# An opening of a trunk layer in written order: modulation weights first, latent blocks of two value heads ahead of the context's, spectra spread anew

## The chip, the core and the metric

The kernel runs on one core of one Trainium2 chip. The core has five engines with instruction streams of their own: TensorE (PE, matmuls), VectorE (DVE), ScalarE (ACT), GpSimd (POOL) and SyncE (SP, which here issues the loads). The metric is the device time of one execution in microseconds (us). A matmul in this kernel multiplies a stationary 128x128 tile with up to 512 moving columns and adds into a bank of PSUM.

## The reference, cut to what matters

One layer of a hybrid block over 512 latent tokens and 256 context tokens of width 1024. What the change touches is the front of it:

```python
mod  = silu(c)     @ w_ada + b_ada          # shift, scale, ... of the latent
modc = silu(c_ctx) @ w_ada + b_ada          # the same of the context
hc = rmsnorm(ctx, norm1_g) * (1 + csc1) + csh1
h  = rmsnorm(x,   norm1_g) * (1 + sc1)  + sh1
khc, vhc, lgc = project_kvg(hc, ...)        # keys, values, gates of the context
kh,  vh,  lg  = project_kvg(h,  ...)        # and of the latent
q = silu(conv(h @ w_in[q] + b_in[q]))       # queries: latent only
# filters of the long convolution, from a small network of sines:
a = sin(fr * (z @ w1 + b1)); a = sin(fr * (a @ w2 + b2)); a = sin(fr * (a @ w3 + b3))
k = (a @ w4) * exp(-t * |decay|);  spec = rfft(k)      # 8 spectra: 2 orders x 4 column groups
```

Behind it follow a chunkwise linear attention (4 heads, both directions), the long convolutions by spectra, gated merge, output projection, SwiGLU and a last norm.

## The kernel before

All large products run in three matmuls: each fp32 operand is split into a high part (ScalarE copy, `hi`) and a low part (VectorE subtraction, `lo`), and hi x hi, lo x hi and hi x lo go to one PSUM bank. In the trace `wr` is a raw weight, `wh` and `wl` its parts, `hTh` and `hTl` the parts of one of the eight modulated latent tiles (128 of 1024 channels x 512 tokens), `hb` among others those of the context.

The opening does this. SyncE loads the vectors (`vecs`), small constants, x in four pieces (`uh`, `ul`), constant matrices (`mats`), the first half of the modulation weights in 16 pieces (`hTh`, `hTl` and `K` lend them their space), later the second half. `ada_first` multiplies a half by silu(c) (L337), copies the sums (L343), transposes them (L346) and adds bias and gain (`modT` L353, `amod` L354). `sq_sums` and `rms_bcast` make the norm: squares on ScalarE, adds on VectorE (L403), column sums (L406), a power on GpSimd (L391), a broadcast product (L393). `modulated` (L1094 to L1100) makes hTh and hTl of four tiles at a time, and `part` the projections of four query tiles, `qps`, with the 24 matmuls of a tile in triples k by k (`gemm`, L233 to L235). `filter_network` (L419 to L438) makes the filters' input, `filter_spectrum` (L453 to L507) one spectrum in three steps: products with w4, window and split; 36 matmuls with a DFT table; combination. `v_head` makes values (and for head 0 the gates, 272 columns) in six blocks of 128 tokens, four latent and two of the context; 24 matmuls each. Then come eight key tiles `k_tile` with the gate arithmetic `gate_math` behind the first.

The order on an engine is set by a scheduler: instructions are taken by priority and by hints (`tc.issue_after`, `tc.high_priority`), each engine runs its own list in that order, and a DMA waits in SyncE's list too. At most eight of SyncE's transfers are in flight; the ninth's issue waits until the first of them has landed.

Of the kernel before, what the change touches and what calls it, by code (L numbers as in the profile page):

```python
# [1 line left out]

# [157 lines left out]
def build(nc, tc, I, out, dbg=None):  # L160
# [33 lines left out]
    NQ, XA, AH, AQ, W0 = 4, (False, False), (2, 2), 2, (3, 0)  # L194
# [6 lines left out]
    def bank(p=None):  # L201
        return T(p or psH, [128, 512], F32, "bank")

# [57 lines left out]
    dma(vecs[:], I["vecs"])  # L261
# [13 lines left out]
    dve.tensor_scalar_mul(mngh[:], mng, 0.5)  # L275
    bhalf = T(P0, [128, 64], F32, "bhalf")
    dve.tensor_scalar_mul(bhalf[:], bin_, 0.5)
# [6 lines left out]
    def ada_prepare(p):  # L284
        nonlocal silc
        silc = T(p, [128, KT, 32], F32, "silc")
# [5 lines left out]
        dve.memset(silc[:], 0.0)  # L292
        dve.scalar_tensor_tensor(silc[:, :, 0:2], th[:], 1.0, cch[:], op0=ALU.add, op1=ALU.mult)
        cb2 = T(p, [128, 40], F32, "cb2")
# [38 lines left out]
    def ada_first(p, half, units, tag):  # L333
        ps = bank()
        for k in range(KT):
# [4 lines left out]
            if k < KT - 1:  # L340
                yield m.ins
        rows = T(p, [128, 512], F32, tag)
        copy = act.activation(rows[:, :256], ps[:, :256], AF.Copy)  # L343
        pt = bank()
        for j in range(2):
            mark = pe.transpose(pt[:, 128 * j : 128 * j + 128], rows[:, 128 * j : 128 * j + 128], ident)  # L346
# [7 lines left out]
        m = dve.scalar_tensor_tensor(amod[:, fs], modT[:, 1, fs], 1.0, n1g[:, fs], op0=ALU.add, op1=ALU.mult)  # L354
        yield mark.ins, m.ins, copy.ins
# [39 lines left out]
    def sq_sums(acc, x, k, nblk, p, tag, ps=None):  # L395
# [8 lines left out]
        if k == KT - 1:  # L404
            for b in range(nblk):
                pe.matmul(ps[:, b : b + 1], acc[:, 128 * b : 128 * b + 128], ones[:, 0:1], start=True, stop=True)  # L406
# [223 lines left out]
    dma(bgb[:], I["bg"].broadcast_to([128, 16]))  # L630

    NV = 258

    def v_weights(h):
        w = 272 if h == 0 else 256
        parts = []
        for kh in range(2):
            src = [(I["wv"][h, kh], slice(0, 256))]
            if h == 0:
                src.append((I["wg"][kh], slice(256, 272)))  # L640
            parts.append(wsplit(src, [128, 4, w]))
        return parts

    def v_head(p, h, parts):
        w = 272 if h == 0 else 256
# [3 lines left out]
        for b0 in range(0, 6, per):  # L649
# [20 lines left out]
            if h == 0:  # L670
                dve.tensor_add(gates[:, b0], ps[:, 256:272], bgb[:])
# [406 lines left out]
    with tc.issue_after(am):  # L1078
        list(e0)
# [530 lines left out]
```

## Time and profile before

| | |
|---|---|
| time, median of 3 runs | 1218.94 us (1218.71 to 1219.33) |
| profiled execution | 1219.83 us |
| its span, first to last instruction | 1218.0 us |
| mean granted TensorE clock | 0.992 |
| TensorE busy | 1180.8 us (97%) |
| VectorE busy | 833.2 us (68%) |
| ScalarE busy | 528.9 us (43%) |

The share of TensorE is an average: it is near 100% over most of the span and far lower in the first 36 us, where data arrive and small chains of steps on several engines precede the first projection. The other engines matter where TensorE waits for them.

### The profile page before, as it was taken

How to read it: one execution, taken by the hardware profiler on the slowest of the kernel's cores; microseconds unless marked ns; L12 is line 12 of the kernel's file. 1: busy time of each engine (PE TensorE's matmuls, PEld its weight loads, DVE VectorE, ACT ScalarE, POOL GpSimd, SP SyncE). 2: the span in 40 equal slices, each digit the busy share in tenths (PEclk: the TensorE clock that was granted, in tenths of full speed). 3: DMA queues.
4: the chain of work that ended last, by engine and by line, in shares of the span. 5: the costliest groups of instructions: out<-in, count | busy, mean ns of one | idle time of the engine just before them, and what ended most of it. 6: DMA issues, size and time to landing. Idle time of an engine off the chain costs nothing.

```text
span 1218.0 us, 16831 instructions
## 1 busy us (share of the span) xinstructions
PE 1180.8 (97%) x6440; PEld 1012.9 (83%) x6440; DVE 833.2 (68%) x1336; ACT 528.9 (43%) x824; POOL 87.7 (7%) x168
## 2 busy tenths in 40 slices
PE   4999999999999999999989999999999999999997
PEld 2799988888888888888778988889888888888886
DVE  5967797978989999897758896767753434432332
ACT  3754465753545444453655642333432232322221
POOL 0011110100010010101032031000000000000000
PEclk9999999999999999999989999999999999999998
DMA  9744453364244353434695686773443333233312
GB/s 346 248 159 163 136 185 106 133 237 143 75 162 137 130 174 102 147 106 155 211 319 180 196 265 218 260 234 121 140 138 104 90 100 101 85 95 96 96 48 70
DMA packets 63377, 189.04 MB, mean 155 GB/s; under 512 B 8760, under 2 KB 12608, under 8 KB 61120
## 3 DMA queue, kind: packets, MB, share of 16 engines
q1 hardware_dynamic: 51536, 150.20, 38.6%
q0 software_dynamic: 11760, 37.76, 8.7%
q8 instruction: 51, 0.84, 0.3%
q14 instruction: 30, 0.25, 0.1%
HBM read 154.37 MB, written 33.55 MB: 154 GB/s over the span
## 4 chain that ended last, share of the span: by engine, by line
PE 89%; DVE 4%; DMA 3%; ACT 2%; issue 1%; POOL 0%; SPq 0%; DVEq 0%; POOLq 0%; ACTq 0%
PE bank L233 26%; PE bank L234 26%; PE bank L235 26%; PE bank L659 2%; PE bank L660 2%; PE bank L661 2%; DMA wr<-qd 1%; DMA wr<-in_wph 1%; PE bank L616 1%; PE bank L463 1%; DVE wl L215 1%; PE bank L464 1%; ACT wh L214 1%; DMA ul<-in_xT 1%; PE bank L337 0%
## 5 line engine op out<-in xcount | busy, mean ns | idle before, releaser
L233 PE MATMUL bank<-hTh,wh 128*128 128x512 f32 (+1 forms) x952 | 366.6, 387 | 2.9 <-ACT hTh L1094 2.0
L234 PE MATMUL bank<-hTl,wh 128*128 128x512 f32 (+1 forms) x952 | 366.1, 386 | 2.9 <-DVE hTl L1100 2.2
L235 PE MATMUL bank<-hTh,wl 128*128 128x512 f32 (+1 forms) x952 | 365.6, 385 | 0.0
L214 ACT ACTIVATE wh<-wr 128x1024 fp32r<-128x1024 f32 (+1 forms) x167 | 172.2, 1033 | 400.8 <-PE bank L234 205.1
L215 DVE TENSOR_TENSOR wl<-wr,wh 128x1024 fp32r<-128x1024 f32 (+1 forms) x167 | 197.8, 1187 | 170.9 <-ACT wh L214 169.6
L233 PEld LDWEIGHTS bank<-hTh,wh 128*128 128x128 f32 x952 | 178.9, 188 | 37.5 <-ACT hTh L1094 2.2
L234 PEld LDWEIGHTS bank<-hTl,wh 128*128 128x128 f32 x952 | 179.0, 188 | 36.8 <-DVE hTl L1100 2.5
L235 PEld LDWEIGHTS bank<-hTh,wl 128*128 128x128 f32 x952 | 179.0, 188 | 34.6
L233 PE MATMUL bank<-big,wh 128*128 128x512 f32 (+1 forms) x266 | 94.7, 356 | 0.0
L234 PE MATMUL bank<-big,wh 128*128 128x512 f32 (+1 forms) x266 | 94.6, 356 | 0.0
L235 PE MATMUL bank<-big,wl 128*128 128x512 f32 (+1 forms) x266 | 94.6, 355 | 0.0
L372 DVE SCALAR_TENSOR_TENSOR wr<-wr,crow 128x1024 f32<-128x1024 f32 x32 | 38.9, 1218 | 28.3 <-DMA wr<-in_wada 28.2
L233 PEld LDWEIGHTS bank<-big,wh 128*128 128x128 f32 x266 | 50.3, 189 | 7.2
L235 PEld LDWEIGHTS bank<-big,wl 128*128 128x128 f32 x266 | 50.3, 189 | 7.1
L234 PEld LDWEIGHTS bank<-big,wh 128*128 128x128 f32 x266 | 50.3, 189 | 7.1
L214 ACT ACTIVATE hb<-hb 128x512 fp32r<-128x512 f32 (+1 forms) x49 | 36.5, 767 | 33.3 <-DVE hb L468 18.5
L1554 DVE TENSOR_TENSOR s<-s,bank 128x512 f32<-128x512 f32 x22 | 15.1, 686 | 46.4 <-PE bank L235 46.4
L391 POOL TENSOR_TENSOR rr<-rv,negh 128x2 f32<-128x2 f32 (+1 forms) x6 | 5.5, 924 | 510.7 <-DVE rv L389 510.7
L215 DVE TENSOR_TENSOR hb<-hb,hb 128x512 fp32r<-128x512 f32 (+1 forms) x49 | 40.4, 858 | 2.0 <-ACT hb L214 1.8
L659 PE MATMUL bank<-wh,hTh 128*128 128x256 f32 (+1 forms) x128 | 36.4, 285 | 0.0
L661 PE MATMUL bank<-wh,hTl 128*128 128x256 f32 (+1 forms) x128 | 36.4, 285 | 0.0
L660 PE MATMUL bank<-wl,hTh 128*128 128x256 f32 (+1 forms) x128 | 36.4, 284 | 0.0
(383 smaller groups left out, 2208.2 us busy)
## 6 DMA issues: line engine op xcount, KB each, us to landing
wr<-in_win SPq DMA_DIRECT2D x64, 512.0 KB, 3.8
wr<-in_w SPq DMA_DIRECT2D x60, 512.0 KB, 3.5
wr<-in_wada SPq DMA_DIRECT2D x32, 512.0 KB, 4.1
Kd<-K POOLq DMA_DIRECT2D x8, 1024.0 KB, 4.7
K<-Kd SPq DMA_DIRECT2D x8, 1024.0 KB, 6.4
wr<-in_wv SPq DMA_DIRECT2D x8, 512.0 KB
gmd<-s POOLq DMA_DIRECT2D x16, 256.0 KB, 2.5
wr<-in_wph SPq DMA_DIRECT2D x8, 512.0 KB, 4.2
```

What stands on the lines that cost most here:

```text
L214: act.activation(hi, x, AF.Copy)
L215: dve.tensor_sub(lo, x, hi.bitcast(F32))
L233: pe.matmul(o, wh, xh, start=first, stop=False)
L234: pe.matmul(o, wh, xl, start=False, stop=False)
L235: return pe.matmul(o, wl, xh, start=False, stop=last)
L372: dve.scalar_tensor_tensor(w, w, 1.0, crow[:], op0=ALU.mult, op1=ALU.mult, accum_out=s)
L463: pe.matmul(ps[:], lhs, w4h, start=True, stop=False)
L464: pe.matmul(ps[:], lhs, w4l, start=False, stop=True)
L659: pe.matmul(o, xh, wh, start=bool(k == 0), stop=False)
L660: pe.matmul(o, xh, wl, start=False, stop=False)
L661: m = pe.matmul(o, xl, wh, start=False, stop=bool(k == KT - 1))
L1554: dve.tensor_tensor(t[:], t[:], pb[:], op=ALU.mult)
```

## The change

Only the opening and the order of value heads and spectra are written anew; the arithmetic is the same, and the number of instructions of each engine too.

- A context manager `in_order` ties the instructions that are traced inside it, engine by engine, into the written order.
- SyncE's list: x and the vectors, constants, the first modulation half, four query weights, the network's weights, the second half, the context, then decay, w4 and DFT table of spectrum 0, then gate bias (`bgb`), value bias and value weights.
- Query projections: in `early_q` a matmul group takes one part of weights and one of hT, for half of the eight tiles; the groups with hTh come first. Weights are split in halves A and B. VectorE makes hTh of tiles 2 and 3. The network's first two layers and the second modulation half stand between these groups.
- The context's squares, norm and modulation are steps (`context`) between the blocks of the value heads. `v_head` is a generator: four latent blocks of head 0, two of head 1, then the context's two blocks of head 0 and one of head 1.
- Spectrum 0 opens behind head 0's last block; spectrum 1 follows at once, 2 in the middle of head 2, 3 and 4 behind heads 2 and 3; query tiles 0 and 1 are finished behind head 2.

```diff
+    @contextmanager
+    def in_order():
+        traced = nc.cur_bb.bb.instructions
+        n, last, ends = len(traced), {}, []
+        yield ends
+        for i in traced[n:]:
+            if i.engine in last:
+                tc.add_manual_dep(
+                    i, last[i.engine], mybir.DependencyInfo(mybir.DependencyClass.NoSync, mybir.DependencyReason.DATA), reason="in_order"
+                )
+            last[i.engine] = i.name
...
-                if half == 0 and (kp, a) == W0:
-                    dma(raws[0][:, :1024].rearrange("p (a b) -> p a b", a=KT), I["win"][FT_Q])
...
-    ada = ada_first(PH, 0, units[0], "s2")
-    for k in range(KT):
-        sq_sums(ax_, xt[k], k, 4, PH, "s2", sums)
-    next(network)
-    ahead(AH[0])
...
-    for i in range(AQ):
-        part(i, 0)
-    next(sp0)
-    ada = ada_first(PH, 1, units[1], "s2")
-    tr, am, copy = ahead(8)
...
+    def early_q(i, ks, w, x):
+        for k in ks:
+            count[i] += 1
+            m = pe.matmul(qps[i][:], early[i][w][:, k], hT[x][k][:], start=count[i] == 1, stop=count[i] == 3 * KT)
...
+    with in_order() as ends:
...
+        units = [ada_load(PH, 0, slots[0])]
+        for i in range(NQ):
+            dma(raws[i], I["win"][FT_Q + i])
+        dma(net[:, :772], I["net"])
+        units.append(ada_load(PH, 1, slots[1]))
...
+        early_q(0, (2, 0, 3, 1), 0, 0)
+        early_q(0, KA, 1, 0)
+        early_q(1, KA, 0, 0)
+        early_q(1, KA, 1, 0)
...
+        network = filter_network(PH, net)
+        next(network)
+        early_q(2, KA, 0, 0)
+        early_q(2, KA, 1, 0)
+        ada = ada_first(PH, 1, units[1], "s2")
...
+        early_q(1, KA, 0, 1)
+        ahead(4)
+        early_q(2, KA, 0, 1)
...
+                dma(bgb[:], I["bg"].broadcast_to([128, 16]))
+                v0 = v_head(PH, 0, v_bias(PH, 0), v_weights(0))
+                raws1, bias1 = v_load(1), v_bias(PH, 1)
...
+        rms_bcast(csums[:, :2], 2, cb_, PH, "s2")
+        next(v0)
+        raws2 = v_load(2)
+        bias2 = v_bias(PH, 2)
+        context(3)
+        next(v0)
+        context(1)
+        next(v0)
+        v1 = v_head(PH, 1, bias1, parts1)
+        context(4)
+        next(v1)
...
-    for h in range(NH):
-        v_head(PH, h, v_weights(h))
-        PR[0] = 600
-        if h:
-            q_late(PH, h - 1)
-        next_spectrum()
+    next_spectrum()
+    for h in range(2, NH):
+        v = v_head(PH, h, bias2, parts2) if h == 2 else v_head(PH, h, v_bias(PH, h), v_weights(h))
+        for i in range(6):
+            next(v)
+            if i == 3:
+                next_spectrum() if h == 2 else None
+        for i in range(2) if h == 2 else (h - 1,):
+            q_late(PH, i)
+        next_spectrum() if h == 2 else next_spectrum()
```

Three places show how the order moves. The first is SyncE's list at its start, before (`in_wada` are the modulation weights, `in_win` query weights, `in_hdec` a spectrum's decay):

```order
1 L261 DMA vecs_69<-in_vecs 128x380
2 L630 DMA bgb_89<-in_bg 128x16
3 L1013 DMA hb_118<-in_net 128x772
4 L1037 DMA uh_134<-in_xT 128x1024
5 L1037 DMA ul_136<-in_xT 128x1024
8 L1040 DMA mats_71<-in_mats 128x640
9 L328 DMA hTh_148<-in_wada 128x512
...
17 L328 DMA K_156<-in_wada 128x512 x4
18 L325 DMA wr_144<-in_win 128x1024
19 L328 DMA K_157<-in_wada 128x512 x4
```

And after:

```order
1 L1111 DMA uh_107<-in_xT 128x1024
2 L1111 DMA ul_109<-in_xT 128x1024
3 L1111 DMA uh_111<-in_xT 128x1024
4 L1115 DMA vecs_69<-in_vecs 128x380
5 L1111 DMA ul_114<-in_xT 128x1024
6 L1116 DMA mats_70<-in_mats 128x640
7 L339 DMA hTh_121<-in_wada 128x512
...
15 L339 DMA K_129<-in_wada 128x512 x4
16 L339 DMA K_130<-in_wada 128x512 x4
17 L1121 DMA wr_117<-in_win 128x1024
...
21 L1122 DMA hb_103<-in_net 128x772
```

The broadcast of the gate bias, the network's weights and the first query weight left the place ahead of the first half's last piece `K`, and four query weights and the network now stand between the halves.

The second is TensorE's list at the first projections, before (L346 transposes of the first half, L233 to L235 projections in triples, with hTh, hTl and `wl` in turn):

```order
24 L346 MATMUL bank_284<-mats_71,s_87_282 128x128 x2
25 L233 MATMUL bank_344<-hTh_320,wh_263 128x512
26 L234 MATMUL bank_344<-hTl_321,wh_263 128x512
27 L235 MATMUL bank_344<-hTh_320,wl_264 128x512
28 L233 MATMUL bank_344<-hTh_326,wh_263 128x512
29 L234 MATMUL bank_344<-hTl_327,wh_263 128x512
30 L235 MATMUL bank_344<-hTh_326,wl_264 128x512
...
108 L233 MATMUL bank_344<-hTh_492,wh_263 128x512
109 L233 MATMUL bank_345<-hTh_492,wh_348 128x512
```

After (L357 transposes, L1093 projections, L433 the network, L348 the second half):

```order
20 L348 MATMUL bank_215<-K_130,silc_104 32x256 x8
21 L357 MATMUL bank_279<-mats_70,s_84_277 128x128 x2
22 L1093 MATMUL bank_287<-hTh_295,wh_299 128x512
...
26 L1093 MATMUL bank_287<-hTh_291,wl_300 128x512
27 L1093 MATMUL bank_287<-hTh_293,wl_300 128x512
...
38 L433 MATMUL bank_348<-hb_103 128x256
...
75 L433 MATMUL bank_402<-hb_347,hb_103 128x256
76 L1093 MATMUL bank_288<-hTl_292,wh_306 128x512
...
80 L348 MATMUL bank_364<-dih_139,silc_104 32x256 x2
...
90 L357 MATMUL bank_432<-mats_70,s_114_430 128x128 x2
91 L1093 MATMUL bank_289<-hTl_292,wh_333 128x512
```

The projections begin with hTh alone, the products with hTl come 45 rows later, the network's first layer stands behind the first 16 projections, and directly ahead of the second half's transposes stand only its own matmuls.

The third is TensorE's list at the value heads, before (first row of a block each; L659 value blocks, with hTh latent and with `hb` context, L463 the products of spectrum 1 with w4, L233 its DFT):

```order
194 L659 MATMUL bank_711<-wh_696,hTh_320 128x272
...
266 L659 MATMUL bank_798<-wh_696,hTh_320 128x272
...
290 L659 MATMUL bank_827<-wh_696,hb_667 128x272
...
314 L659 MATMUL bank_856<-wh_696,hb_667 128x272
...
338 L463 MATMUL bank_898<-wh_891,astack_353 128x512
...
346 L659 MATMUL bank_941<-wh_928,hTh_320 128x256
...
442 L659 MATMUL bank_1045<-wh_928,hb_667 128x256
...
490 L233 MATMUL bank_1105<-hb_921,dfh_120 128x256
```

After (L689 value blocks, L420 and L404 the context's norm, L436 the network's third layer, L477 spectrum 0's products, L248 its DFT):

```order
147 L689 MATMUL bank_585<-wh_514,hTh_291 128x272
...
195 L420 MATMUL bank_528<-mats_70,s_69_193 128x1 x2
...
220 L404 MATMUL bank_529<-mats_70,rr_675 128x128 x2
...
221 L689 MATMUL bank_700<-wh_514,hTh_291 128x272
...
245 L689 MATMUL bank_749<-wh_577,hTh_291 128x256
...
293 L436 MATMUL bank_800<-hb_347,hb_103 128x256 x2
...
342 L689 MATMUL bank_874<-wh_514,hb_575 128x272
...
390 L477 MATMUL bank_942<-hb_871,astack_865 128x512
...
446 L689 MATMUL bank_1119<-wh_932,hTh_291 128x256
...
474 L248 MATMUL bank_1027<-hb_1019,dfh_105 128x256
```

Head 1's latent blocks (`wh_577`) now stand ahead of the context blocks of head 0 (`wh_514` with `hb`), and spectrum 0 behind them, inside the heads.

## Rows read from the trace of the kernel before

**Rows 1.** From the page: busy us, share and instructions; TensorE's 40 slices, in tenths
```profile
PE 1180.8 (97%) x6440; PEld 1012.9 (83%) x6440; DVE 833.2 (68%) x1336; ACT 528.9 (43%) x824; POOL 87.7 (7%) x168
...
PE   4999999999999999999989999999999999999997
```

**Rows 2.** Busy time by stretch: length, each engine, PEclk, DMA share, GB/s
```profile
0.00:33.00 33.00, 13.18 (x92) 7.73 (x93) 20.47 (x50) 13.40 (x21) 1.32 (x6) 0.99 0.96 349
33.00:36.00 3.00, 3.00 (x9) 2.36 (x9) 2.97 (x5) 2.96 (x6) 0.00 (x0) 0.57 1.06 388
10.00:30.00 20.00, 11.18 (x89) 6.76 (x89) 14.48 (x32) 7.45 (x13) 1.01 (x1) 1.00 1.04 398
0.00:240.00 240.00, 219.02 (x1532) 194.47 (x1533) 190.25 (x357) 135.08 (x217) 22.77 (x46) 0.99 0.54 186
```

**Rows 3.** Waits of TensorE to 250 us: total, times, longest
```profile
PE bank L406 <- DVE s L403: 8.3, 1, 8.3
...
PE bank L234 <- DVE hTl L1100: 2.2, 1, 2.2
...
PE bank L796 <- DVE hb L793: 0.6, 1, 0.6
```

**Rows 4.** The chain of waits through the opening: start, length, what
```profile
28.09 0.43 DVE hb L430
```

**Rows 5.** Single instructions in order of time: start, length, what, wait
```profile
3.31 0.22 ACT L289 ACTIVATE cth<-vecs 128x16 f32<-128x16 f32 x1 [1.29 <-DMA vecs<-in_vecs]
...
6.72 1.22 PE L419 MATMUL bank<-hb 66*128 66x256 f32 x2 [6.72 <-DMA hb<-in_net]
...
23.05 1.13 PE L422 MATMUL bank<-hb,hb 128*128 128x256 f32 x4
...
24.80 2.10 PE L337 MATMUL bank<-K,silc 128*32 128x256 f32 x31
...
25.18 1.95 SPq L328 DMA_DIRECT2D hTh<-in_wada  x4
...
27.45 0.44 PE L346 MATMUL bank<-mats,s 128*128 128x128 f32 x2 [0.56 <-ACT s L343]
...
29.03 1.52 ACT L1094 ACTIVATE hTh<-uh,modT,amod 128x512 fp32r<-128x512 f32 x2 [1.63 <-DVE amod L354]
...
29.90 0.49 PE L233 MATMUL bank<-hTh,wh 128*128 128x512 f32 x1 [2.00 <-ACT hTh L1094]
30.05 1.00 DVE L1099 TENSOR_SCALAR s<-uh,amod,modT 128x512 f32<-128x512 f32 x2
...
35.91 0.39 PE L233 MATMUL bank<-hTh,wh 128*128 128x512 f32 x1
...
36.14 0.39 PE L234 MATMUL bank<-hTl,wh 128*128 128x512 f32 x1
```

**Rows 6.** The DMA queue's GB/s, first 10 us in 40 slices
```profile
GB/s 0 0 0 0 0 0 0 140 152 294 201 86 68 79 75 150 210 362 419 358 410 307 377 279 229 262 229 295 328 393 393 410 426 360 393 410 360 361 361 442
```

**Rows 7.** TensorE's instructions where the second half and head 0 begin
```profile
44.06 1.07 PE L337 MATMUL bank<-hTh,silc 128*32 128x256 f32 x16
...
47.65 0.50 PE L233 MATMUL bank<-hTh,wh 128*128 128x512 f32 x1
...
62.93 0.28 PE L233 MATMUL bank<-hb,dfh 128*128 128x256 f32 x1
...
67.14 0.29 PE L659 MATMUL bank<-wh,hTh 128*128 128x272 f32 x1
```

**Rows 8.** Busy time by stretch, head 0 to the gates
```profile
150.00:185.90 35.90, 35.38 (x224) 31.37 (x222) 34.22 (x69) 22.28 (x38) 5.12 (x10) 1.00 0.52 177
67.14:185.87 118.73, 118.21 (x888) 112.80 (x886) 91.96 (x154) 59.58 (x94) 15.55 (x29) 1.00 0.47 158
```

**Rows 9.** VectorE's groups by shape, 67 to 190 us
```profile
L465 DVE TENSOR_TENSOR hb<-bank,hb 128x512 f32<-128x512 f32 x16 | 10.3, 681 | 0.3
...
L506 DVE TENSOR_TENSOR K<-hb 128x1024 f32<-128x1024 f32 x5 | 6.1, 1217 | 0.0
```

More of the change, by code (lines that the diff above doesn't have):

```diff
@@ L1 @@
 import math
+from contextlib import contextmanager
 import numpy as np
@@ L403, in sq_sums, with column_sums @@
             dve.tensor_add(acc[:, :n], acc[:, :n], sq[:, :n])
-        if k == KT - 1:
-            for b in range(nblk):
-                pe.matmul(ps[:, b : b + 1], acc[:, 128 * b : 128 * b + 128], ones[:, 0:1], start=True, stop=True)
+        if k == KT - 1 and ps is not None:
+            column_sums(acc, nblk, ps)
+    def column_sums(acc, nblk, ps):
+        for b in range(nblk):
+            pe.matmul(ps[:, b : b + 1], acc[:, 128 * b : 128 * b + 128], ones[:, 0:1], start=True, stop=True)
     def filter_network(p, net):
@@ new lines, in modulated, with early_hi @@
+    def modulated(k, hi_dve=False):
+        for i, t in enumerate(("hTh", "hTl")):
+            hT[i].append(T(PT, [128, SEQ], F32R, t))
+        return modulate(xt[k], hT[0][k][:], hT[1][k][:], k, 0, hi_dve)
+    early, count = [], [0] * NQ
+    def early_hi(i, ks):
+        if len(early) <= i:
+            early.append([v[:, :1024].rearrange("p (a b) -> p a b", a=KT) for v in (T(PW, [128, WMAX], F32R, t, 4) for t in ("wh", "wl"))])
+        act.activation(early[i][0][:, ks], raws[i][:, ks], AF.Copy)
@@ L1052, in ahead @@
-        return m
-    for k in range(KT):
-        sq_sums(ax_, xt[k], k, 4, PH, "s2", sums)
-    next(network)
-    ahead(AH[0])
-    xb = bank()
-    rms_bcast(sums[:, :4], 4, xb, PH, "s2")
-    next(network)
-    ahead(AH[1])
-    for k in range(4):
-        dve.tensor_tensor(xt[k], xt[k], xb[:], op=ALU.mult)
-    early = []
-    def early_split(i):
-        raw, *hl = [
-            v[:, :1024].rearrange("p (a b) -> p a b", a=KT) for v in (raws[i], T(PW, [128, WMAX], F32R, "wh", 4), T(PW, [128, WMAX], F32R, "wl", 4))
-        ]
-        first = act.activation(hl[0], raw, AF.Copy).ins
-        early.append(hl)
-        yield first
-        dve.tensor_sub(hl[1], raw, hl[0].bitcast(F32))
@@ L1075, in build @@
-    e0 = early_split(0)
-    with tc.issue_after(next(e0)):
-        tr, am, copy = ahead(8 - AH[0] - AH[1])
-    with tc.issue_after(am):
-        list(e0)
-    dec, skip = spectrum_vectors(PH, *sp[0])
-    dma(w4r, I["hw4"][sp[0]].rearrange("p f n -> p (f n)"))
-    for i in range(1, NQ):
-        dma(raws[i][:, :1024].rearrange("p (a b) -> p a b", a=KT), I["win"][FT_Q + i])
-    dma(fr, I["dftf"])
-    units.append(ada_load(PH, 1, slots[1]))
-    t = T(PH, [128, KT, CTX], F32, "K")
-    dma(t[:], I["cxT"])
@@ L1088, in build @@
-    for k in range(KT):
-        cxt.append(t[:, k])
-    hT = ([], [])
-    def modulate(x, hi, lo, k, i, on_act):
-        a_, b_ = amod[:, k, i : i + 1], modT[:, 0, k, i : i + 1]
-        high = act.activation(hi, x, AF.Identity, bias=b_, scale=a_).ins
-        t = x if on_act else T(PH, [128, 512], F32, "s2")[:, : x.shape[-1]]
-        if on_act:
-            act.activation(t, x, AF.Identity, bias=b_, scale=a_)
-        else:
-            dve.tensor_scalar(t, x, a_, b_, op0=ALU.mult, op1=ALU.add)
-        return high, dve.tensor_sub(lo, t, hi.bitcast(F32)).ins
@@ L1102, in modulated @@
-    def modulated(p):
-        for k in range(4 * p, 4 * p + 4):
-            for i, t in enumerate(("hTh", "hTl")):
-                hT[i].append(T(PT, [128, SEQ], F32R, t))
-            low = modulate(xt[k], hT[0][k][:], hT[1][k][:], k, 0, XA[p])
-        return low
-    def part(i, p):
-        gemm(qps[i], *early[i], *hT, SEQ, range(4 * p, 4 * p + 4))
-        if p:
-            act.activation(qb[i], qps[i][:], AF.Identity, bias=bin_[:, FT_Q + i : FT_Q + i + 1])
-    high, low = modulated(0)
```

273 lines of the change are left out of this document (196 added, 77 removed).

## The prediction

> **What bounds the kernel now.** I read first the page's engine shares and slices, then the busy time by stretch, then the waits of TensorE, then the chain of waits through the opening, and last single instructions. TensorE is busy 1180.8 of 1218.0 us and its slices read 9 everywhere but in the first, in two or three of the middle and in the last [rows 1]. The profiled execution took 1219.83 us, 1.8 more than its span, and 0.9 more than the median of the three timed runs, 1218.94. So everything that does not start TensorE earlier, or keep it from waiting, is off the path.
>
> The change rewrites the program up to about 270 us; from there on the order of TensorE is the old one. In 0 to 240 us TensorE is busy 219.0 us: of the 21 missing, 19.8 are in the first 33 us [rows 2]. Its waits say the same: the longest is for the adds of the squares, the one just before the projections run for hTl of the first modulated tiles (2.2), and later the gate arithmetic holds TensorE 0.6 at L796 [rows 3]. And in 33 to 36 us TensorE is busy 3.00 us at a granted clock of 0.57, between its two levels, with nine matmuls where thirteen of 0.23 us would fit [rows 2, 5]. So there are two things to win, an earlier first projection matmul (29.90 us) and fewer holes behind it. The chain of waits shows what the 29.90 hangs on: the filter network's last VectorE step ends at 28.52, modT follows it directly, then amod, hTh and hTl [rows 4]. The other arm is the modulation weights, whose last matmuls (31 from 24.80, 2.10 us) end at 26.90 [rows 5].
>
> **The change, part by part.**
>
> *DMA order.* The 8 KB broadcast of the gate bias, the network's weights (0.39 MB) and the first query weight (0.52 MB) no longer stand ahead of the modulation weights' first half. The last of that half lands at 25.18: the queue has eight transfers in flight, and the issue at 25.18 is the one eight behind it [rows 5]. In 10 to 30 us the queue moves 398 GB/s [rows 2], so 0.92 MB less is 2.3 us. The quarter-microsecond slices of the first 10 us show a hole from 2.50 to 4.25 us, seven slices with a mean of 124 GB/s, right where the broadcast's small packets follow the vectors: 1.75 x (1 - 124/398) = 1.2 us lost [rows 6]; and network and broadcast land 3.4 us behind the vectors (6.72 against 3.31) where 1.0 would do at 398 GB/s [rows 5]: 2.4. That goes too: between 0 and 2.4 us, I take 1.6, nearer the slices. The half lands at 25.18 - 2.3 - 1.6, say 21.2 (20.5 to 22.9).
> The Trainium skill, page "DMA: Bandwidth & Descriptors", section "Anatomy of one DMA", gives each DMA a fixed cost of about 2 us, mostly the receipt of its last bytes. If that time blocked the queue, the 8 KB transfer alone would give back 2.0, and if transfers in flight hide it, nothing; the eight in flight and the slices speak for something between.
>
> *From the landing to the first projection matmul.* Now 25.18 to 29.90, 4.7 us. TensorE had a backlog (the 31 half-matmuls, 0.068 each), since network matmuls stood between; behind it came the copy, two transposes, and modT, held 0.4 by the network's vector steps [rows 4, 5]. Afterwards the network stands behind the first projections, so from 21.2: the last eight half-matmuls 0.54, copy with its gaps 0.55, transposes 0.44, modT and amod 0.51 (28.52 to 29.03), and hTh, whose tile 2 VectorE now makes, 0.5 (its 512-column tensor_scalar, 1.00 for two) [rows 4, 5]: 23.7. First matmul at 23.9, 6.0 earlier. The latent norm does not bind: x is now first in the queue, and its sums and norm stand between the modulation's matmuls, behind weights that land by 16.
>
> *Holes behind it.* Now nine matmuls need 29.90 to 35.91 = 6.0 us where 9 x 0.228 = 2.05 would do: 3.96 lost [rows 5], to the wait for hTl and to the low clock. Afterwards the matmuls that need only hTh and the weights' high parts come first; hTh 0 and 1 come from ScalarE at 0.76 each [rows 5], so the first four reach 25.15 where 24.8 would do: 0.35 lost. Then weights are late. The second modulation half now moves among the projections; behind 21.2 the queue brings four query weights (2.10 MB), the network (0.39) and that half (4.19), 6.69 MB at 388 to 398 GB/s [rows 2]: its last weights land at 38.0 to 38.4. TensorE reaches them at 23.9 + 40 x 0.228 + 0.35 + 3.2 of modulation (56 of 64 half-matmuls at 0.056, from 44.06 to 47.65 before [rows 7]) + 1.1 of network = 37.7, and waits up to 0.9. The copy ahead of its transposes has no cover now (before, other projections stood there): 0.55. Sum 1.8 lost against 3.96: 2.1 gained.
>
> *Work that only changes place.* The network's matmuls move behind the first projection: four single ones at 0.28 and four more in two pairs, 8 x 0.28 = 2.3 us of TensorE [rows 5] that then stand in the saturated stretch: -2.3. Spectrum 0, the context's column sums and its norm leave the projections for the value heads; they stood in the saturated stretch before as well: 0. Opening in sum: 6.0 + 2.1 - 2.3 = 5.8 us earlier.
>
> *Low clock.* The same hole in front of the first projection (copy, transposes, modT: 2 us) stays, so the low level may come again: at the lower level a matmul takes about twice its 0.228, so 0 to 8 x 0.228 = 1.8 us for the same eight or nine, of which the wait for the second half takes back up to 0.9. I take 0.5. By the Trainium skill, page "TensorE: Matmul & The Clock Gate", Part 1, the throttled clock is the default and activity lifts it; so a start without it would be luck, and the sum by that page would carry about 1 instead of 0.5. The trace agrees that the low level came behind the hole (0.86, then 0.57 [rows 2]), though 0 to 20 us show 1.00 on little work.
>
> *Value heads, context, spectra.* The latent blocks of heads 0 and 1 come first, 4 x 24 x 0.124 + 2 x 48 x 0.117 = 23.1 us of TensorE (256 columns: 36 from 62.93 to 67.14, 0.117 each; 272 in proportion [rows 7]), so the context's chain (squares, column sums, norm, 16 activations, 8 subtractions) has cover; each step is written between blocks and may wait by 0.2 to 0.6 us at four places (column sums behind the last square; the network's sine behind the context's ScalarE steps; spectrum 0's first accumulation; a block behind the subtractions). From the value heads to the gates VectorE is now busy 91.96 of 118.73 us, 34.2 of 35.9 in the last stretch [rows 8]. It gets the rest of spectrum 0 (11.4 less 3.8 done later anyway; 4 x 0.68 + 2 x 1.22 + 2.43 + 1.36 + 2.43 [rows 9]) and the context's products, 8 x about 0.4: about 103 of 126.5, 82%. On average it fits; but three spectra fall into heads 2 and 3, where the old order had two, and there the spectra's steps come 0 to 1.5 us ahead of their use. I take 1.4 for all new waits together, between 0 (each covered) and 4 (each of eight places 0.5).
>
> *Gates.* The wait at L796, and a smaller one at L756, stay in kind, since VectorE's rows ahead of them are the same: 0, from -0.5 to +0.7.
>
> Sum on the profiled execution: 1219.83 - 5.8 + 0.5 + 1.4 = 1215.9; on the median of the runs, 0.9 lower, **1215.0 us**, 0.32% faster.
>
> **Rivals.**
>
> *VectorE takes the gain back.* If its saturated stretch in heads 2 and 3 (95% busy already [rows 8]) stalls each of four spectra by 1 us, and the gates wait 1 more, the new waits are 5 and not 1.4: 1218.6, no change. For it: the thin leads; against it: 20% slack on average, and 40 us of k tiles behind head 3.
>
> *The opening comes less early.* The half lands at 22.9 (the broadcast was not the hole), nine matmuls run at the low clock (1.8) and the second half's weights come at 40: 5.8 - 1.7 - 1.3 - 1.0 = 1.8 earlier, less 1.4: 1218.5. For it: rows of the clock; against it: the slices show the hole where the broadcast is. Milder, with one of the three, it is 1216.5.
>
> *Late value weights (slower).* In-order chains let nothing pass a late arrival. Head 0's weights stand behind bgb, the bias and between two gate-weight pieces, all small packets, in one queue. By bytes they land near 48 to 50, and the projections end at 52.6. If each of four small transfers costs what I read at the start, 1.6 to 2.4, they land at 56 to 58; with 2.3 for the first high and low parts the heads start at 58 to 60: 5.5 to 7.5 lost, 1220.5 to 1222.5. It costs nothing until they land after 50.3, and decides the sign from about 54.
>
> *The order does not do what it says* (the chains move nothing on the chip, since an engine runs its rows in order anyway): excluded; the rows of TensorE and SyncE show the moves.
>
> **How the numbers follow.** A change below 0.2% (2.4 us) can't be told from none here. Forecast 0.55 (its own range 1213 to 1216.8, as the landing goes by +-1, clock by +-0.7, waits by +-1.2); VectorE 0.13; opening less early 0.19, half of it milder; late weights 0.09; still faster, below 1212.5 (no new wait, no low clock, full broadcast gain: 1215.0 - 0.5 - 1.4 - 0.8 = 1212.3 or less) 0.04. Faster by over 0.2% is below 1216.5: 0.93 of the forecast, a half of the mild rival, the last: 0.60; slower, above 1221.4: 0.07 of the late weights (where the splits of the next heads come late behind them, 2 to 4 us more) and 0.03 of the VectorE rival (stalls of 2 us each, not 1): 0.10; no change the remaining 0.30. The range leaves out 0.1 at either end: 1212 to 1219.6.
>
> **What would show it.** Right: the last weights of the first half near 21, first projection matmul near 24, no DVE wait of 2 us behind it, projections done near 53, value heads at once; waits of TensorE in 50 to 200 us of 2.5 us in sum. Wrong: a first matmul after 26; a clock near 0.5 for more than 4 us; a TensorE wait for wh of L214 at the start of head 0; waits for VectorE of more than 4 us between 85 and 190 us; gates reached less than 3 us earlier than 185.87.

## The result and the profile after

The changed kernel is slower, by a ratio of 1.0017 to the kernel before (95% interval 1.0009 to 1.0025), about 2.1 us on 1218.94; the prediction of 1215.0 and its range, up to 1219.6, were both below it. The medians of 14 runs each are 1221.62 and 1219.77 us. The profiled execution took 1222.04 us, its span is 1220.2.

The page of the changed kernel, its engine shares and TensorE's slices; to be set beside [rows 1]:

```profile
PE 1184.5 (97%) x6440; PEld 1014.0 (83%) x6440; DVE 836.6 (69%) x1342; ACT 529.6 (43%) x826; POOL 87.8 (7%) x168
...
PE   5999999999999999999989999999999999999997
```

The first slice has gone from 4 to 5, so the opening is fuller, and yet TensorE's busy time is 3.7 us longer for the same 6440 instructions. (VectorE and ScalarE show six and two more than before, where the section on the change has them equal: four splits go in halves now, and VectorE makes hTh of two tiles in ScalarE's place.) The next view is busy time by stretch of the changed kernel, columns as in [rows 2]:

```profile
0.00:33.00 33.00, 19.86 (x118) 11.77 (x119) 18.05 (x42) 12.36 (x20) 1.32 (x6) 0.95 0.97 362
33.00:36.00 3.00, 3.00 (x26) 1.79 (x25) 2.90 (x8) 0.42 (x1) 0.00 (x0) 1.00 1.06 386
...
0.00:240.00 240.00, 221.55 (x1517) 194.18 (x1518) 187.75 (x356) 132.62 (x214) 23.03 (x46) 0.99 0.53 184
```

In 0 to 33 us TensorE is busy 19.86 us where it was 13.18; in 33 to 36 it runs at a granted clock of 1.00 where it was 0.57. Of these 6.7 us only 2.5 are left at 240 us (221.55 against 219.02), and with them fewer instructions have run by then, 1517 where it was 1532, so even these are longer ones or slower ones rather than work ahead. So the opening did as it should, and something between 36 and 240 us takes all of it back. TensorE's waits from 50 to 275 us in the changed kernel (total, times, longest) name it:

```profile
PE bank L248 <- ACT hb L229: 2.7, 3, 1.0
PE bank L436 <- ACT hb L446: 1.4, 1, 1.4
PE bank L828 <- DVE hb L825: 0.5, 1, 0.5
PE bank L788 <- DVE hb L787: 0.2, 1, 0.2
```

Before, that stretch held TensorE only at the gates, at L796 [rows 3] and here:

```profile
PE bank L756 <- DVE hb L755: 0.5, 1, 0.5
```

L788 and L828 are the same gate lines now. New are the first matmul of a spectrum's DFT (L248), three times behind ScalarE's rounding to the high part (L229), and the network's third layer (L436).

From one matmul on, TensorE's order is the same in both kernels. It starts at 273.48 us before and at 274.39 in the changed kernel, 0.91 late; the experiments come back to it as the common matmul. The sum up to there, from the starts of TensorE's instructions against the usual step of their shape: by 60 us about 5.0 are gained; the new waits with the steps behind them cost 5.1; the gates give back 0.46 (0.33 + 0.70 against 0.68 + 0.81); and some 480 matmuls of 256 columns (288 of the DFTs, 192 of the context's part of the key tiles) step by 0.120 us and no longer by 0.117, 1.4 us.

### The profile page after: what moved, and what is told of

It reads as the page before. It is cut to its first block, busy times and chain, and to the rows that moved or that the text cites. A ratio compares the mean times of both kernels' runs of the same rounds, so it can differ in the third digit from the quotient of the medians.

```text
span 1220.2 us, 16838 instructions
## 1 busy us (share of the span) xinstructions
PE 1184.5 (97%) x6440; PEld 1014.0 (83%) x6440; DVE 836.6 (69%) x1342; ACT 529.6 (43%) x826; POOL 87.8 (7%) x168
## 4 chain that ended last, share of the span: by engine, by line
PE 85%; DVE 5%; DMA 4%; ACT 3%; issue 1%; POOL 0%; SPq 0%; DVEq 0%; POOLq 0%; ACTq 0%
PE bank L248 25%; PE bank L249 25%; PE bank L250 25%; PE bank L1093 2%; PE bank L690 1%; PE bank L691 1%; PE bank L689 1%; DMA wr<-in_wph 1%; ACT wh L229 1%; DVE wl L230 1%; PE bank L630 1%; DMA fd<-in_hdec 1%; DMA wr<-qd 1%; DMA mats<-in_mats 1%; DMA hTl<-in_wada 0%
## 5 line engine op out<-in xcount | busy, mean ns | idle before, releaser
L248 PE MATMUL bank<-hTh,wh 128*128 128x512 f32 (+1 forms) x920 | 353.8, 386 | 0.9 <-ACT hTh L1648 0.9
L249 PE MATMUL bank<-hTl,wh 128*128 128x512 f32 (+1 forms) x920 | 352.8, 385 | 0.6 <-DVE hTl L1649 0.6
L250 PE MATMUL bank<-hTh,wl 128*128 128x512 f32 (+1 forms) x920 | 352.7, 384 | 0.0
L229 ACT ACTIVATE wh<-wr 128x1024 fp32r<-128x1024 f32 (+2 forms) x167 | 172.1, 1033 | 376.6 <-PE bank L249 194.7
L230 DVE TENSOR_TENSOR wl<-wr,wh 128x1024 fp32r<-128x1024 f32 (+2 forms) x167 | 197.8, 1188 | 154.3 <-ACT wh L229 153.3
L248 PEld LDWEIGHTS bank<-hTh,wh 128*128 128x128 f32 x920 | 172.6, 188 | 33.7 <-ACT hTh L1648 1.3
L250 PEld LDWEIGHTS bank<-hTh,wl 128*128 128x128 f32 x920 | 172.6, 188 | 33.4 <-DVE wl L230 0.2
L249 PEld LDWEIGHTS bank<-hTl,wh 128*128 128x128 f32 x920 | 172.6, 188 | 33.3 <-DVE hTl L1649 0.8
L248 PE MATMUL bank<-big,wh 128*128 128x512 f32 (+1 forms) x266 | 94.7, 356 | 0.0
L248 PEld LDWEIGHTS bank<-big,wh 128*128 128x128 f32 x266 | 50.3, 189 | 7.2
L229 ACT ACTIVATE hb<-hb 128x512 fp32r<-128x512 f32 (+1 forms) x49 | 36.3, 767 | 25.9 <-DVE hb L564 10.4
L689 PE MATMUL bank<-wh,hTh 128*128 128x256 f32 (+1 forms) x128 | 36.6, 287 | 0.0
```

The lines of the kernel that those rows point to most:

```text
L229: act.activation(hi, x, AF.Copy)
L230: dve.tensor_sub(lo, x, hi.bitcast(F32))
L248: pe.matmul(o, wh, xh, start=first, stop=False)
L249: pe.matmul(o, wh, xl, start=False, stop=False)
L250: return pe.matmul(o, wl, xh, start=False, stop=last)
L689: pe.matmul(o, xh, wh, start=bool(k == 0), stop=False)
```

## The experiments

### The network's third layer earlier

At 74.94 us TensorE waits for the sine of the network's second layer. The sine stands on ScalarE behind the context's work. The changed kernel, ScalarE and TensorE there:

```profile
73.98 0.60 ACT L1242 ACTIVATE K<-K,modT,amod 128x256 f32<-128x256 f32 x1
...
74.49 0.40 ACT L446 ACTIVATE hb<-hb 128x256 f32<-128x256 f32 x1
...
74.94 1.13 PE L436 MATMUL bank<-hb,hb 128*128 128x256 f32 x4 [1.43 <-ACT hb L446]
```

The last of the context's ScalarE steps begins at 73.98, the sine directly behind it, and the matmul behind the sine. So the experiment lets the network go ahead of the context's steps:

```diff
         rms_bcast(csums[:, :2], 2, cb_, PH, "s2")
+        next(network)
         next(v0)
...
         context(1)
-        next(network)
         next(v1)
```

> The changed kernel with one step moved: the filter network's third layer (sine, two matmul pairs, six VectorE steps) is written right behind the context norm's broadcast and so ahead of the context's 16 ScalarE steps, not behind them. Theory (the opening wins 5.0 us, and TensorE's new waits for ScalarE steps behind longer queues give it back): the wait of TensorE for the sine (1.4, with its cold start 2.0) goes and nothing takes its place, since the context's last tile ends near 77.5 and is needed near 80; 1.4 to 2.0 us less than the changed kernel, so about +0.0 to +0.6 against before. Rival (VectorE is the bound there, waits only move): the wait before spectrum 0's DFT at 99.7 grows by what this one loses; 0 to 0.5 us less than the changed kernel.

Measured: 1.0009 (1.0000 to 1.0019) to the kernel before, by the ratios 1.0 us below the changed kernel, but the two intervals overlap. The wait at L436 is gone, and the other one has grown from 2.7. Its waits of TensorE, and the stretch behind the longest of them by busy time and clock:

```profile
PE bank L248 <- ACT hb L229: 4.3, 3, 2.0
```

```profile
181.00:186.00 5.00, 4.51 (x21) 4.16 (x22) 4.83 (x7) 3.78 (x6) 0.80 (x2) 0.66 0.21 79
```

The same stretch of the changed kernel:

```profile
181.00:186.00 5.00, 4.18 (x31) 4.01 (x32) 4.96 (x7) 4.07 (x7) 0.99 (x3) 1.00 0.20 77
```

Behind a wait of 2.0 us the granted clock is 0.66 in the mean, and 21 instructions run where 31 did. The common matmul starts at 275.86 us in this profile, 1.47 later than in the changed kernel (274.39). So no gain is shown for this edit alone. That the wait only moves is what the rival said, though its reason, VectorE, is not shown by it: TensorE came sooner to spectra that were no sooner ready.

### A second buffer for the decay

Why are the spectra late? The changed kernel around 99.7 us, from the exponentials of spectrum 0 to the DFT of the same spectrum, with the next one's decay load between them:

```profile
90.29 2.56 ACT L474 ACTIVATE hb<-fd,vecs 128x512 f32<-128x512 f32 x4
...
92.88 0.33 SPq L462 DMA_DIRECT2D fd<-in_hdec  x1
...
96.35 0.63 ACT L457 ACTIVATE fd<-fd 128x512 f32<-128x512 f32 x1 [1.66 <-DMA fd<-in_hdec]
96.89 0.61 ACT L229 ACTIVATE wh<-wr 128x512 fp32r<-128x512 f32 x1
...
97.53 0.69 DVE L230 TENSOR_TENSOR wl<-wr,wh 128x512 fp32r<-128x512 f32 x1 [0.96 <-ACT wh L229]
...
98.58 2.01 ACT L229 ACTIVATE hb<-hb 128x1024 fp32r<-128x1024 f32 x2 [1.08 <-DVE hb L483]
...
99.69 0.74 PE L248 MATMUL bank<-hb,dfh 128*128 128x256 f32 x4 [0.87 <-ACT hb L229]
```

The decay (`fd`) has one buffer. Its load for the next spectrum is issued at 92.88, when the four exponentials that read the old one have ended (90.29 + 2.56), and the absolute value of the new one starts at 96.35. ScalarE runs its rows in order and idles 1.66 us in front of it; the high part of the next spectrum's weight, VectorE's low part, the last step of spectrum 0's filter and the high part that TensorE needs all queue behind. The same happens ahead of the other two waits, with VectorE as the middle link: at 175.13 it has stood idle for ScalarE, and from there it works without a break to the filter's last step.

```profile
173.52 0.63 ACT L457 ACTIVATE fd<-fd 128x512 f32<-128x512 f32 x1 [2.17 <-DMA fd<-in_hdec]
...
175.13 1.23 DVE L230 TENSOR_TENSOR wl<-wr,wh 128x1024 fp32r<-128x1024 f32 x1 [1.48 <-ACT wh L229]
...
181.82 0.74 PE L248 MATMUL bank<-hb,dfh 128*128 128x256 f32 x4 [1.02 <-ACT hb L229]
...
217.48 0.63 ACT L457 ACTIVATE fd<-fd 128x512 f32<-128x512 f32 x1 [2.43 <-DMA fd<-in_hdec]
...
227.17 0.74 PE L248 MATMUL bank<-hb,dfh 128*128 128x256 f32 x4 [0.78 <-ACT hb L229]
```

The first of the three stands in head 2, which begins at 95.30 us. The others, of spectra 4 and 5, stand among the key tiles: head 3's last block starts at 149.63.

But ScalarE waited for this load before as well. Its row for it in 50 to 240 us, of the kernel before and of the changed one:

```profile
ACT fd L443 <- DMA fd<-in_hdec: 10.0, 5, 3.4
```

```profile
ACT fd L457 <- DMA fd<-in_hdec: 11.8, 6, 2.5
```

So the theory is that the wait for the load reaches TensorE only now, since the spectra come shortly ahead of their use. The edit gives the decay two buffers and loads it one spectrum earlier, ScalarE's place for the absolute value kept (and silu(c) borrows the space of the tile that later holds the network's output):

```diff
-    BUFS = {"hb": 6, "K": 2, ...
+    BUFS = {"fd": 2, "hb": 6, "K": 2, ...
...
-        dec, skip = spectrum_vectors(p, o, c)
-        act.activation(dec[:], dec[:], AF.Abs)
+        with tc.issue_after(exps[-2] if len(exps) > 1 else abs0[0]):
+            dec, skip = spectrum_vectors(p, o, c)
+        with tc.issue_after(exps[-1]):
+            act.activation(dec[:], dec[:], AF.Abs)
```

> The changed kernel with two buffers for a spectrum's decay vector instead of one, so that its load is issued one spectrum earlier; the order of TensorE stays the same to the row, VectorE's in all but two rows. Theory: ScalarE waits 1.7, 2.2 and 2.4 us for that load at 96, 173 and 217 us, in order, ahead of weight splits that hold VectorE and so the high parts for which TensorE waits (1.0, 1.2 and 0.9 with restarts); these waits shrink to under 0.3 each, 2.0 to 3.0 us less than the changed kernel, -1.0 to 0.0 against before. Rival (VectorE's own work is the bound in heads 2 and 3): TensorE's waits at 182 and 227 stay within 0.2, at most 0.5 us less.

Measured: 0.9991 (0.9982 to 1.0001), 3.2 us below the changed kernel by the ratios, whose intervals do not meet. The common matmul starts at 271.84, 2.55 earlier than in the changed kernel; of these about 0.3 come from the granted clock in the opening, as shown further down. Its largest waits of TensorE from 50 to 275 us:

```profile
PE bank L436 <- ACT hb L446: 1.4, 1, 1.4
PE bank L420 <- DVE s L414: 0.6, 1, 0.6
PE bank L834 <- DVE hb L831: 0.5, 1, 0.5
```

All three waits of the spectra are gone, so VectorE's own work was not their bound. One of 0.6 for the context's squares (L420) has come; why was not followed.

### Both

```diff
+    BUFS = {"fd": 2, ...            # and the loads as above
...
+        next(network)
         next(v0)
```

> Both edits, the network's third layer early and two decay buffers. Theory: the savings add, since they are waits at different places of one saturated engine: 3.5 to 5.0 us less than the changed kernel, 1.5 to 3.0 us less than before. Rival (VectorE is the bound): less than 1 us below the changed kernel, so still slower than before by about 1.

Measured: 0.9976 (0.9965 to 0.9988), 0.41% under the changed kernel. Its largest waits:

```profile
PE bank L834 <- DVE hb L831: 0.5, 1, 0.5
PE bank L420 <- DVE s L414: 0.5, 1, 0.5
PE bank L248 <- ACT hb L229: 0.4, 1, 0.4
```

From the second buffer alone to both is 0.15%, 1.8 us, by the ratios, which their intervals do not resolve. By the profiles the common matmul comes 0.64 us earlier (271.20 against 271.84), or 1.0 counted from the first value block, which came 0.39 later here (54.49 against 54.10). So the network's move, of which no gain was shown alone, is worth about 1.0 us in this order once the spectra are ready in time, still less than the 2.0 of its wait; 0.4 of the rest is the new wait at L248. At the common matmul this kernel is 2.28 us ahead of the kernel before, the changed one 0.91 late.

### The same two buffers in the kernel before

If the single buffer cost the kernel before anything too, the gain would say nothing of the change. The edit is the one above, in the kernel before, with three small tiles put into other tiles' room.

```diff
+    BUFS = {"fd": 2, ...
...
+        with tc.issue_after(exps[-2] if len(exps) > 1 else exps[-1]):
+            dec, skip = spectrum_vectors(p, o, c)
```

> The kernel before with two buffers for the decay vector (three small vectors take borrowed space for it). Its ScalarE waits for the decay loads as well, 10.0 us in five waits up to 240 us. Theory (the single buffer costs only where the spectra stand too close to their use, so it is part of what the change does): TensorE of before had no wait for a spectrum's parts, so nothing to win, within 0.5 us of before. Rival (two buffers are a gain by themselves, in either order): 2 to 3 us faster than before.

Measured: 1.0011 (1.0000 to 1.0021): no gain, and 1.3 us more where "within 0.5" was expected. TensorE's waits from 50 to 275 us are the two at the gates, 0.6 each, as in the kernel before, and ScalarE's wait for the load is gone. So there was no wait of TensorE to win, and the price of the single buffer belongs to the new order.

What this kernel is slower by is another thing. The first matmul of spectrum 0's DFT and the first of head 0, with 36 steps between them:

```profile
62.89 0.28 PE L233 MATMUL bank<-hb,dfh 128*128 128x256 f32 x1
...
67.21 0.29 PE L665 MATMUL bank<-wh,hTh 128*128 128x272 f32 x1
```

These are 0.120 us each, where [rows 7] has 0.117 for the same matmuls. Up to there the rows of TensorE, VectorE and ScalarE stand in the same order as in the kernel before; what the edit has changed is where tiles lie and, from 48 us on, the order of SyncE's loads. So the 0.120 of the changed kernel, too, need not come from the new order of its matmuls. The common matmul starts 0.99 us later than before here (274.47), and 480 such steps are worth 1.4.

### The kernel before once more

The same program a second time; nothing is edited.

> The kernel before once more, for a second profile. In the two profiles so far the changed kernel is 0.9 us later than before at 273 us, and 2.5 later at 715 us, though its instructions are the same from 273 us on. Theory: these 1.6 us are differences between executions (waits at the state stage of 1.6 against 1.9 and such); a second profile of before moves by up to 1.5 us in the same stretch against the first. Rival: they are a later effect of the change; the second profile of before agrees with the first within 0.3 us all along.

Measured: 1218.11 us, span 1216.2, 1.8 below the first profile of the same program. Up to 525 us the two agree within 0.2 us from 40 us on; by 648 us the second is 1.9 ahead. TensorE's largest wait in 540 to 720 us, for VectorE, was 3.8 us in the first and 2.9 in the second, and the granted clock behind it differs. The stretch in the first profile and in the second:

```profile
629.00:637.00 8.00, 6.59 (x21) 5.47 (x22) 7.08 (x15) 3.64 (x4) 4.46 (x9) 0.57 1.14 372
```

```profile
629.00:637.00 8.00, 7.36 (x37) 6.44 (x38) 7.91 (x14) 4.91 (x6) 3.68 (x7) 0.79 1.16 387
```

At 0.57 there ran 21 matmuls, at 0.79 it was 37. So two executions of one program differ there by 2 us, and the changed kernel's profile, whose lateness grows from 0.91 at 273 us to 2.5 at 715, can't tell what of the part behind 525 us is the change. The theory holds for that part, and the rival for a small one: from 273 to 525 us the changed kernel falls 0.6 us further behind, where the second profile of before moves by less than 0.1. Profiles are compared up to 273 us here, and totals by the timed ratios.

### The value heads' blocks unchained

A rival says that the tie to the written order is the price, since the scheduler would place the steps better.

```diff
-    with in_order():
+    with ExitStack():
         for i in (0, 1):
```

> The changed kernel with the second in-order section, the one of the value heads and the context's steps, left to the scheduler's priorities. Theory (what holds TensorE is how late a spectrum's steps stand and the decay load, not the chaining): the waits before spectrum DFTs and the network's sine stay about as they are, within 1.5 us of the changed kernel. Rival (chains let one late load hold everything behind it): the waits at 74.9 and 99.7 go, 2 to 3 us faster than the changed kernel.

Measured: 1.0054 (1.0041 to 1.0067), slower by more than was expected either way. L436 does not wait, but the spectra do:

```profile
PE bank L248 <- ACT hb L229: 6.9, 3, 3.4
```

The rival falls: without the ties TensorE waits still longer for the spectra's steps.

### The spectra apart

Another rival puts the price down to crowding: three spectra in heads 2 and 3. Here the one in the middle of head 2 goes, and one more runs beside the k tiles.

```diff
-            if i == 3:
-                next_spectrum() if h == 2 else None
...
-        if ft in (0, 2, 4, 6):
+        if ft in (0, 2, 4, 6, 7):
```

> The changed kernel with spectrum 2 opened behind head 2 and not in its middle, and so every later spectrum one place later (3 behind head 3, 4 to 7 at key tiles 0, 2, 4, 6, the last closed behind tile 7). One decay buffer, network late, as in the changed kernel. Theory A (spectra stand too close in heads 2 and 3, and VectorE is the bound there): the waits before the DFTs at 182 and 227 us shrink under 0.5 together, 1.5 to 2.5 us less than the changed kernel. Theory B (the single decay buffer alone makes them, wherever the spectra stand): a wait of 1 us each stays with the spectra that moved; within 0.7 us of the changed kernel.

Measured: 1.0006 (0.9997 to 1.0015), 0.11% under the changed kernel, which the overlapping intervals do not resolve; by the profiles it is 0.5 us earlier at 274 us. So the profile has the time of theory B and the waits of theory A. TensorE's largest waits from 50 to 275 us are these, and two at the gates of 0.8 and 0.6; then ScalarE's for the load:

```profile
PE bank L436 <- ACT hb L446: 1.4, 1, 1.4
PE bank L248 <- ACT hb L229: 1.2, 1, 1.2
```

```profile
ACT fd L457 <- DMA fd<-in_hdec: 10.4, 5, 2.9
```

Of the spectra's three waits only the first (100.08 us) is left, though ScalarE still waits 10.4 us for the loads. So the load's wait alone does not hold TensorE, and crowding alone does not either (with two buffers the crowded order has no such wait): it takes both, a thin lead and a step in order in front of it that waits.

### Two refinements of the best

First, in the version with both edits, the context's last squares one block earlier (for the wait at L420) and the second spectrum's decay loaded earlier (for L248):

```diff
+        sq_sums(ac_, cxt[KT - 1], KT - 1, 2, PH, "s2", None)
         parts1 = v_split(raws1, 1)
...
+        ready[sp[1]] = decay_load(PH, *sp[1])
         context(3)
```

> The best so far (network's third layer early, two decay buffers) with two places mended that came up in its profile: the context's last square ahead of head 1's weight splits, so that the column sums don't wait 0.5 for VectorE, and spectrum 1's decay loaded behind the value weights and not ahead of them. Theory: 0.5 to 1.0 us less, 0.995 to 0.997 of before. Rival (the value weights' landing sets head 0 anyway, or the wait moves on): within 0.3 of it.

Measured: 0.9981 (0.9969 to 0.9993), above the 0.995 to 0.997 that was expected and not told from the version with both edits alone. L420 does not wait any more, but TensorE waits 1.4 us at L248, and ScalarE ahead of it for a store that frees a buffer:

```profile
178.30 0.69 ACT L627 ACTIVATE s<-bank,vecs 128x512 f32<-128x512 f32 x1 [1.42 <-DMA kd<-s]
```

Second, both edits and the spectra apart:

```diff
+    BUFS = {"fd": 2, ...            # and the network ahead, as above
...
+        if ft in (0, 2, 4, 6, 7):
```

> Network's third layer early, two decay buffers, and spectra one place later. Theory A: the last wait before a DFT (0.6 at 179) goes, 0.3 to 1 us less than with the first two edits, about 0.997 of before or below. Theory B: the two edits had taken what there was; within 0.5 us of them.

Measured: 0.9975 (0.9966 to 0.9985), median 1215.25 us: the lowest of all, 0.25% below the kernel before, though not told apart from the version without the spread. From 50 to 275 us TensorE waits only at the gates, 0.6 and 0.5.

### The broadcast back in front

The last one prices a term of the opening: the 8 KB broadcast of the gate bias goes back among the loads of x.

```diff
+            if q == 0:
+                dma(bgb[:], I["bg"].broadcast_to([128, 16]))
...
-                dma(bgb[:], I["bg"].broadcast_to([128, 16]))
```

> The changed kernel with the 8 KB broadcast of the gate bias put back to the front of the queue, as its second transfer; nothing else moves. It measures the one term of the opening that was taken between bounds. By my working the first modulation half lands 1.6 us later than the changed kernel's 21.0 (0 to 2.4), and the first projection at 26.0 and not 24.4. By the fixed cost of a DMA blocking the queue 2.0; if eight transfers in flight hide a small one, 0.1.

Measured in one run: 1225.41 us. The first projection, and the queue's GB/s in 40 slices of the first 10 us:

```profile
GB/s 0 0 0 0 0 0 0 246 279 295 344 295 295 182 118 20 37 3 3 4 19 69 166 313 394 360 410 442 377 459 377 405 381 368 457 400 444 418 405 414
```

```profile
26.46 1.67 PE L1093 MATMUL bank<-hTh,wh 128*128 128x512 f32 x4 [1.34 <-DVE hTh L1065]
```

The changed kernel has no such hole:

```profile
GB/s 0 0 0 0 0 0 0 213 115 213 328 262 328 311 262 295 377 475 344 426 344 426 459 344 442 304 305 352 426 390 393 426 391 426 363 395 395 324 287 320
```

From 3.25 to 5.5 us the queue moves 3 to 182 GB/s, and the first projection comes 2.06 us later than in the changed kernel (24.40). The prediction took 1.6 for this term. The Trainium skill, page "DMA: Bandwidth & Descriptors", section "Anatomy of one DMA", has a fixed cost of about 2 us, told there of DMAs issued by GpSimd and put down mostly to the receipt of a DMA's own last bytes. The 2.06 of this case is of that size, but it is a load of SyncE's, and the slices show that the transfers behind it in the queue were held, so the agreement does not show that cost at work.

By the common matmul (278.38) this run is 3.99 us behind the changed kernel, so nearly as much again was lost behind the opening, most of it in TensorE's waits for the spectra (2.7 in the changed kernel). Why they grew was not followed:

```profile
PE bank L248 <- ACT hb L229: 4.5, 3, 2.0
```

## Why the prediction was wrong

The opening came as worked out. The last weights of the first half landed at 21.1 (21.2 was forecast), and the changed kernel's TensorE and VectorE show the rest:

```profile
22.63 0.44 PE L357 MATMUL bank<-mats,s 128*128 128x128 f32 x2 [0.47 <-ACT s L354]
...
23.71 1.00 DVE L1065 TENSOR_SCALAR hTh<-ul,amod,modT 128x512 fp32r<-128x512 f32 x2
...
24.40 1.62 PE L1093 MATMUL bank<-hTh,wh 128*128 128x512 f32 x3 [1.33 <-DVE hTh L1065]
...
54.45 0.28 PE L689 MATMUL bank<-wh,hTh 128*128 128x272 f32 x1
```

TensorE waits 0.47 us for the copy ahead of the transposes and, for the second half, 0.50 (0.55 each was forecast); the first projection starts at 24.40 (23.9); the second half's weights hold nobody (up to 0.9 was allowed). The low clock came again and no milder. Four microseconds of the kernel before, of the changed one, and of the one with two decay buffers, whose opening is the same and ran at 1.00:

```profile
32.00:36.00 4.00, 3.39 (x9) 2.75 (x10) 3.97 (x6) 3.96 (x7) 0.00 (x0) 0.57 1.05 386
```

```profile
24.00:28.00 4.00, 3.60 (x9) 2.92 (x10) 3.88 (x8) 3.98 (x8) 0.00 (x0) 0.57 1.03 398
```

```profile
24.00:28.00 4.00, 3.69 (x15) 2.91 (x16) 3.88 (x8) 3.98 (x8) 0.00 (x0) 1.00 1.03 397
```

From the first projection to the first value block the changed kernel takes 30.05 us and the last one 29.79 (24.31 to 54.10), so the low clock cost about 0.3 where 0.5 was forecast.

In all, about 5.0 us were gained by 60 us; the forecast was 5.8 less 0.5 for the clock, 5.3. Value heads start at 54.45 and wait for no weights, so the rival of late value weights fell; "the opening comes less early" fell too, since its first matmul would have been past 26. The gates gave 0.46, within the 0.5 that was allowed. One of the signs can't be read: the gates are reached at 198.73 us, later than the 185.87 of before, because the new order puts 74 more matmuls ahead of them, about 13 us of TensorE.

**The step that failed** is "I take 1.4 for all new waits together". They cost 5.1: 2.0 at the network's third layer and 1.0, 1.2 and 0.9 at three spectra. This is beyond the bound of 4 that the step gave itself, and about the size of the first rival, "VectorE takes the gain back" (5). That the sizes agree is luck: the rival had four spectra at 1 us and 1 at the gates, and measured were three spectra with 3.1 in sum, 2.0 at the network's third layer, and less at the gates than before. Nor was its place right. It looked at heads 2 and 3 and counted the key tiles behind head 3 as slack, and two of the three waits stand among the key tiles. What stood in front was the order of ScalarE's rows: a load into a single buffer, issued only behind the buffer's last reader, stood ahead of the chain that the spectra need, through VectorE, and the context's steps stood ahead of the network's sine. The prediction had counted VectorE's share (82%) and had not looked at ScalarE's wait for `fd`, 10.0 us in the trace of before. There it cost nothing, as the waits of TensorE with two buffers in the kernel before show; in the new order it cost about 2.3 us by the profiles, the clock's share taken off, and 3.2 by the ratios. The prediction also counted the sine behind the context's steps as one wait of 0.2 to 0.6; it took 2.0.

The second miss is a term that was not in the sum: 1.4 us for 256-column matmuls. The changed kernel's DFT of spectrum 0, with 24 steps between these two rows, and the clock of that stretch at 1.00:

```profile
102.54 0.28 PE L248 MATMUL bank<-hb,dfh 128*128 128x256 f32 x1
...
105.42 0.28 PE L248 MATMUL bank<-hb,dfh 128*128 128x256 f32 x1
```

2.88 us for 24 are 0.120 each; in [rows 7] 36 took 0.117 each. The kernel before with two decay buffers has 0.120 as well, so it does not take the new order of the matmuls; what makes it stays open. The sum of the profiled execution up to 273 us then closes: forecast 3.9 early; 3.7 more of waits, 1.4 of slower matmuls, 0.3 less of the opening and 0.5 of the gates make 1.0 late, and 0.91 was measured. Without the slower steps the same sum is 0.4 early, about as fast as before; the waits took the gain, and it took the slower steps too to make it late. Two readings of the prediction are off and carry nothing: one slice of the middle is under 9 in [rows 1], not two or three, and the clock of 0.86 is not among [rows 2].

## What to carry to other kernels

Where work is moved closer to its use, it isn't enough to add up how busy its engine is: follow the chain back through every engine that runs it in order, and price each wait that stands in front of it there, even one that cost nothing before. A buffer that is loaded only behind its last reader makes such a wait; a second one costs 256 KB here and took back 2 to 3 us. When two waits follow one another, taking away the first alone can show nothing of what it is worth. And an edit that only makes room moves tiles: compare the steps of the same matmuls before putting a difference down to the order.

## What the runs showed of the hardware

- An 8 KB broadcast to 128 partitions left the queue at 3 to 182 GB/s for over 2 us and put off the first projection behind it by 2.06 us, in one run.
- Behind a TensorE wait of 2.0 us the granted clock was 0.66 in the mean over 181 to 186 us; behind waits of 1.0 it stayed at 1.00 in the same stretch. The Trainium skill, page "TensorE: Matmul & The Clock Gate", Part 1, has the lower clock as the default that activity lifts; the first agrees, and the second shows that a short wait need not bring it. Nor does the length of the wait settle it: the run with the broadcast in front waited 1.98 us at the same DFT and stayed at 1.00:

```profile
185.15 0.74 PE L248 MATMUL bank<-hb,dfh 128*128 128x256 f32 x4 [1.98 <-ACT hb L229]
```

```profile
185.00:190.00 5.00, 4.85 (x36) 4.67 (x37) 5.00 (x7) 4.07 (x9) 0.80 (x2) 1.00 0.21 79
```

- 256-column matmuls of the DFT stepped by 0.117 us in both profiles of the kernel before, and by 0.120 in the changed kernel, in the versions with both edits and in the kernel before with two decay buffers, at a granted clock of 1.00. In this last one TensorE, VectorE and ScalarE run their rows up to the first DFT in the order of the kernel before, so that order does not make the 0.003 us. The places of tiles or SyncE's loads may; neither was tried.
- Two executions of one program differed by 1.9 us between 525 and 648 us, with a wait of 3.8 against 2.9 us and a granted clock of 0.57 against 0.79 over 629 to 637 us, and with none of the difference where the change is.
